# A pool for the rows of v opened ahead of the gates' pool, gathers from the seventh block on, and one low part of u in five on GpSimd

## The chip, the cores and the metric

The kernel runs on one core of a Trainium2 chip. The metric is the device time of one execution in microseconds (us); the time of the kernel before is the median of three runs. One more execution was taken by the profiler, and all rows below are from it.

## The reference

Two transformer blocks run one after the other on 512 tokens of width 1024 in fp32. The change lies in the second half of the first block, a product-key mixture of experts: each token picks 8 x 16 of 16384 single-neuron experts, weighs each expert's answer by gelu(u . h) times a softmax gate, and adds up the rows of v.

```python
def peer_ffn(h, w_query, sub_keys, peer_u, peer_v):
    ...
    idx = (jnp.take_along_axis(i1, ci // PEER_TOPK, axis=-1) * PEER_N_KEYS
           + jnp.take_along_axis(i2, ci % PEER_TOPK, axis=-1))
    g = jax.nn.softmax(sc, axis=-1)
    u_sel = peer_u[idx]
    act = jax.nn.gelu(jnp.einsum('chkd,cd->chk', u_sel, hc), approximate=False) * g
    v_sel = peer_v[idx]
    return jnp.einsum('chk,chkd->cd', act, v_sel)
    ...
```

## The kernel before

The kernel has three parts: a first mixer block, the mixture of experts (class `Peer`), and two layers of a second kind of block. The change touches only `Peer`, about 290 to 1680 us of the span.

For 384 of the 512 tokens (`ND`) the experts are computed densely, as matrix products over all 16384 experts in 128 blocks of 128 experts. For the other 128 tokens (`NGT`) the rows of u and v that a token has picked are gathered from DRAM, one gather of 128 rows of u and v for each of the 128 picks of a token.

An fp32 product is made of three products of rounded parts: an operand x is split into a high part (ScalarE, called ACT, rounds it) and a low part (x minus the high part, on VectorE, called DVE, or on GpSimd, called POOL). TensorE (PE) then multiplies high by high, high by low and low by high.

`Peer.run` opens pools one after the other. Pools are placed on a stack, so a pool that is opened after another is closed takes the same memory.

- `norm` and `route` (pool `pr`) normalize the tokens and pick the experts.
- `gates` (pool `pg`) makes a dense table of gate values. For each group of four tokens, 96 groups in all, it builds two sets of comparison matrices: `gb` (one tile for four tokens, made by DVE in two groups of three, L1774, and by GpSimd in the third, in four instructions, L1772) and `ga` (one tile for each token, made by DVE, L1784, or by ACT in two steps, L1781 and L1782). PE multiplies them (L1786, eight records in the profile for a group), ACT copies the result to `gst` (L1787), and after eight groups SP writes `gst` to DRAM (L1788), 12 times in all. `gb` has 3 buffers, `ga` 8, `gst` 2.
- `scores(b)` makes gelu(u . h) of block b for the dense tokens: SP loads `wr` (L1798), the high part `wh` is made by ACT (L1800; by DVE in one block of four from 34 on), the low part `wl` by GpSimd for b < 28 and by DVE from then on (L1802). 24 matmuls of 384 columns (L209 to L211, output `S`) follow, and ACT applies the gelu into a tile `big` (L1809), of which there are 36. 34 blocks are made ahead of the experts (`AHEAD`). Their tiles come from pools that are open all the time.
- `experts` (pool `pw`, which takes the memory of `pg`) runs over the 128 blocks: `gate(b)` loads the gates of four blocks at a time as `gt` (L1815), multiplies the scores by them on DVE (L1818) and splits the product into `ah` and `al` (L194, L195). SP loads 128 rows of v as `vr` (L1837), ACT makes `vh` (L1840), GpSimd `vl` (L1841). Then the next one or no block of scores is made, then 18 matmuls of 512 columns add to the output (L1850, output `V`), then a share of the gathers is issued: GpSimd sends the gather (L1914, `rows`, 3 buffers), DVE multiplies the u half by the token and sums (L1916), ACT and DVE make the weight (L1920, L1921), and DVE adds the v half to `acc` (L1923).

The gathers are spread evenly over the blocks up to six before the end (`LAST`): after block b, (b + 1) x 128 / 122 of them have been issued.

The order in which each engine takes its instructions is set when the program is compiled. The compiler's scheduler goes by the order of the program, but lets an engine take a later instruction whose inputs and buffers are there when an earlier one isn't ready; on the chip each engine, and each DMA queue, then keeps to that order. A tile of a pool that was opened on memory of a closed pool waits for that pool.

Of the kernel before, what the change touches and what calls it, by code (L numbers as in the profile page):

```python
# [9 lines left out]
F32 = mybir.dt.float32  # L10
F32R = mybir.dt.float32r
I32 = mybir.dt.int32
# [7 lines left out]
P = 128  # L20
D = 1024
# [235 lines left out]
class Block1:  # L257
# [29 lines left out]
    def big(self, name, dt=F32):  # L287
        return self.p.tile([P, NCH * 528], dt, tag="x16", name=self.net.nm(name), bufs=3)
# [1302 lines left out]
NG4 = ND // 32  # L1591
AHEAD = 34
LAST = 6
BIGS = 36
ON_ACT = (1,)

# [9 lines left out]
class Peer:  # L1606
# [3 lines left out]
    def run(self):  # L1610
        net, nc, tc = self.net, self.nc, self.tc
        with ExitStack() as c0:
            self.p = c0.enter_context(tc.tile_pool(name="pp", bufs=1))
            net.load_cst1(self.p, 128)
            with ExitStack() as c1:
                self.w = c1.enter_context(tc.tile_pool(name="pr", bufs=2))
                net.nsc = 3
                self.norm()
                self.route()
            with ExitStack() as c1:  # L1620
                self.w = c1.enter_context(tc.tile_pool(name="pg", bufs=2))
                self.gates()
            self.s = {}
            for b in range(AHEAD):
                self.scores(b)
            with ExitStack() as c1:
                self.w = c1.enter_context(tc.tile_pool(name="pw", bufs=2))
                self.experts()
# [99 lines left out]
    def gates(self):  # L1728

        net, nc, p, w = self.net, self.nc, self.p, self.w  # L1730
        V = nc.vector
        ident, iota = net.c("ident"), net.c("iota")
        self.gd = net.dram.tile([NG4, P, P, 32], F32, name="gates")

        g = self.sc
        gT = w.tile([P, 4, P], F32, tag="gT", name="gT", bufs=1)
        iT = w.tile([P, 2, 4, P], F32, tag="iT", name="iT", bufs=1)
        nT = w.tile([P, 2, 4, P], F32, tag="nT", name="nT", bufs=1)
        for i in range(4):
            mx = w.tile([P, 8, 1], F32, tag="rsm", name=net.nm("rmx"))  # L1740
            V.tensor_copy(mx, g[:, i, :, 0:1])
            V.tensor_tensor(g[:, i], g[:, i], mx.to_broadcast([P, 8, 16]), op=OP.subtract)
            nc.scalar.activation(g[:, i], g[:, i], AF.Exp)
            sm = w.tile([P, 8], F32, tag="rsm", name=net.nm("rsm"))
            V.tensor_reduce(sm, g[:, i], axis=AX.X, op=OP.add)
            V.reciprocal(sm, sm)
            V.tensor_tensor(g[:, i], g[:, i], sm.unsqueeze(2).to_broadcast([P, 8, 16]), op=OP.mult)
        self.g = g
        for i in range(4):
            with net.banks("pb", "gt"):  # L1750
                ps = net.ps()
            nc.tensor.transpose(ps[:, :P], g[:, i].rearrange("p a b -> p (a b)"), ident)
            nc.tensor.transpose(ps[:, P:2 * P], self.ex[:, i].rearrange("p a b -> p (a b)"), ident)
            nc.scalar.activation(gT[:, i], ps[:, :P], AF.Copy)
            xi = w.tile([P, 3, P], I32, tag="xi", name=net.nm("xi"))
            V.tensor_copy(xi[:, 0], ps[:, P:2 * P])
            V.tensor_scalar(xi[:, 1], xi[:, 0], 7, None, op0=OP.logical_shift_right)
            V.tensor_scalar(xi[:, 2], xi[:, 0], 127, None, op0=OP.bitwise_and)
            V.tensor_copy(iT[:, :, i], xi[:, 1:3])
            nc.gpsimd.tensor_scalar(nT[:, 0, i], iT[:, 0, i], -1.0, None, op0=OP.mult)  # L1760
            nc.gpsimd.tensor_scalar(nT[:, 1, i], gT[:, i], -1.0, None, op0=OP.mult)
        for t0 in range(0, ND, 32):
            st = w.tile([P, P, 32], F32, tag="gst", name=net.nm("gst"))
            for t4 in range(t0, t0 + 32, 4):
                with net.banks("pd", "G"):
                    ps = net.ps()

                i, j4 = divmod(t4, P)
                b = w.tile([P, 4, P], F32, tag="gb", name=net.nm("gb"), bufs=3)
                if t4 // 4 % 3 == 2:  # L1770
                    for t in range(4):
                        nc.gpsimd.tensor_scalar(b[:, t], iota, iT[:, 1, i, j4 + t:j4 + t + 1], None, op0=OP.is_equal)  # L1772
                else:
                    V.tensor_tensor(b, iota.unsqueeze(1).to_broadcast([P, 4, P]),  # L1774
                                    iT[:, 1, i, j4:j4 + 4].unsqueeze(2).to_broadcast([P, 4, P]), op=OP.is_equal)
                pt = ps.rearrange("p (k t) -> p t k", t=4)
                for t in range(4):
                    j = j4 + t
                    a = w.tile([P, P], F32, tag="ga", name=net.nm("ga"), bufs=8)
                    if t in ON_ACT:  # L1780
                        nc.scalar.activation(a, iota, AF.Abs, bias=nT[:, 0, i, j:j + 1])  # L1781
                        nc.scalar.activation(a, a, AF.Relu, bias=gT[:, i, j:j + 1], scale=nT[:, 1, i, j:j + 1])  # L1782
                    else:
                        V.tensor_scalar(a, iota, iT[:, 0, i, j:j + 1], gT[:, i, j:j + 1], op0=OP.is_equal,  # L1784
                                        op1=OP.mult)
                    nc.tensor.matmul(pt[:, t], b[:, t], a, start=True, stop=True)  # L1786
                nc.scalar.activation(st[:, :, t4 - t0:t4 - t0 + 4], ps.rearrange("p (k t) -> p k t", t=4), AF.Copy)  # L1787
            nc.sync.dma_start(self.gd[t0 // 32], st)  # L1788


    def big(self, dt=F32):
        return self.p.tile([P, 384], dt, tag="big", name=self.net.nm("big"), bufs=BIGS)

    def scores(self, b):

        net, nc, p = self.net, self.nc, self.p
        raw = net.wt("wr")
        nc.sync.dma_start(raw, self.A["ut"][b])  # L1798
        uh, ul = net.wt("wh"), net.wt("wl")
        (nc.vector.tensor_copy(uh, raw) if b % 4 == 3 and b >= AHEAD else nc.scalar.activation(uh, raw, AF.Copy))  # L1800
        e = nc.gpsimd if b < 28 else nc.vector
        e.tensor_tensor(ul, raw, uh.bitcast(F32), op=OP.subtract)  # L1802
        with net.banks("pa", "S"):
            ps = net.ps()[:, :ND]
        for c in range(NCH):
            cs = slice(c * P, (c + 1) * P)
            net.mm3(ps, (uh[:, cs], ul[:, cs]), (self.xh[c][:, :ND], self.xl[c][:, :ND]), c == 0, c == NCH - 1)
        self.s[b] = self.big()[:, :ND]
        nc.scalar.activation(self.s[b], ps, AF.Gelu)  # L1809
# [15 lines left out]
    def experts(self):  # L1825

        net, nc, w, hT = self.net, self.nc, self.w, self.hT
# [4 lines left out]
        done, got = AHEAD, 0  # L1832
        slots = NGT
        for b in range(P):
            ah, al = self.gate(b)
            raw = w.tile([P, D], F32, tag="vr", name=net.nm("vr"), bufs=2)
            nc.sync.dma_start(raw, self.A["uv"][b * P:(b + 1) * P, D:])  # L1837
            vh = w.tile([P, D], F32R, tag="vh", name=net.nm("vh"), bufs=2)
            vl = w.tile([P, D], F32R, tag="vl", name=net.nm("vl"), bufs=2)
            nc.scalar.activation(vh, raw, AF.Copy)  # L1840
            nc.gpsimd.tensor_tensor(vl, raw, vh.bitcast(F32), op=OP.subtract)  # L1841
            while done < min(P, AHEAD + (b + 1) * (P - AHEAD) // (P - LAST)):
                self.scores(done)
                done += 1
            for i, ps in enumerate(out):
                ts = slice(i * P, (i + 1) * P)
                for k in range(2):
                    cs = slice(k * 512, (k + 1) * 512)
                    for n, (x, y) in enumerate(((ah, vh), (ah, vl), (al, vh))):
                        nc.tensor.matmul(ps[k], x[:, ts], y[:, cs], start=b == 0 and n == 0, stop=b == P - 1 and n == 2)  # L1850
            n = min(slots, (b + 1) * slots // (P - LAST)) - got
            while n > 0:
                self.gather(got, min(n, 3))
                got, n = got + min(n, 3), n - 3
# [123 lines left out]
```

## Time and profile before

| | us |
|---|---|
| median of three runs | 3770.8 |
| the three runs | 3761.55, 3776.63, 3770.8 |
| the profiled execution, its own time | 3765.66 |
| its span, from the first to the last instruction | 3763.8 |

| engine | busy us | share of the span |
|---|---|---|
| PE, matmuls | 3593.1 | 95% |
| PE, weight loads | 2972.0 | 79% |
| DVE | 2592.4 | 69% |
| ACT | 1412.5 | 38% |
| POOL | 1087.1 | 29% |

The profile is one execution taken by the hardware's profiler. Busy time of PE is modelled and overlaps, so a busy PE need not be at its peak. "PEclk" is the clock granted to PE as a share of the full clock, and "DMA" the mean busy share of the core's 16 DMA engines. A row that ends in "<-" and a name tells how long the engine stood idle before an instruction and what ended the idle time.

### The profile page before, as it was taken

What the parts mean: (1) busy time and instruction counts of PE and PEld (TensorE: products, weight loads), DVE (VectorE), ACT (ScalarE), POOL (GpSimd) and SP (SyncE); (2) the same over time, 40 slices, a digit from 0 to 9 for tenths busy, and PEclk for the clock granted to TensorE, in tenths of its full rate; (3) what the DMA queues carried; (4) which work ended last, traced back from release to release, by engine and by line L of the source; (5) the groups of instructions that cost most, each with busy time, mean ns of one, the idle gap of its engine ahead of it and who ended that gap; (6) DMA issues with size and microseconds to landing.
All of it is one profiled execution on the core that took longest, in us unless ns stands there. A gap on an engine that the chain in (4) does not pass through costs nothing. (4 is left out here: it accounts for less than half of the span.)

```text
span 3763.8 us, 46084 instructions
## 1 busy us (share of the span) xinstructions
PE 3593.1 (95%) x17229; PEld 2972.0 (79%) x17229; DVE 2592.4 (69%) x4504; ACT 1412.5 (38%) x2405; POOL 1087.1 (29%) x685
## 2 busy tenths in 40 slices
PE   7798979889999999999999899999999998999999
PEld 6656878878889988888887667888888875668887
DVE  9668999788888889854445987444444459975443
ACT  3253259423333333342223446322322234453222
POOL 4424767445555555530002222000100012210000
PEclk8899989999999999999999999999999999999999
DMA  4212225888888888833223111323332321112233
GB/s 119 78 40 94 76 91 224 284 304 295 286 307 292 301 291 297 301 111 95 93 98 94 64 46 56 96 95 95 96 95 95 98 93 54 46 45 95 95 96 101
DMA packets 181520, 529.88 MB, mean 141 GB/s; under 512 B 22256, under 2 KB 73008, under 8 KB 163120
## 3 DMA queue, kind: packets, MB, share of 16 engines
q1 hardware_dynamic: 157504, 388.64, 31.0%
q0 software_dynamic: 19392, 136.06, 9.8%
q10 hardware_dynamic: 4400, 2.24, 0.3%
q8 instruction: 136, 2.23, 0.2%
q14 instruction: 88, 0.72, 0.1%
HBM read 495.52 MB, written 30.18 MB: 140 GB/s over the span
## 5 line engine op out<-in xcount | busy, mean ns | idle before, releaser
L1027 ACT ACTIVATE wh<-wr 128x1024 fp32r<-128x1024 f32 (+1 forms) x334 | 347.4, 1040 | 1029.8 <-PE ps L210 766.0
L210 PE MATMUL ps<-x,wh 128*128 128x512 f32 x1408 | 548.8, 390 | 2.1 <-DVE x L996 2.0
L209 PE MATMUL ps<-x,wh 128*128 128x512 f32 x1408 | 549.1, 390 | 0.0
L211 PE MATMUL ps<-x,wl 128*128 128x512 f32 x1408 | 547.9, 389 | 0.0
L1028 DVE TENSOR_TENSOR wl<-wr,wh 128x1024 fp32r<-128x1024 f32 (+1 forms) x288 | 344.4, 1196 | 78.0 <-ACT wh L1027 71.1
L1008 POOL TENSOR_TENSOR s<-s,s 128x512 f32<-128x512 f32 x42 | 67.0, 1596 | 1125.2 <-ACT s L1006 1113.9
L1841 POOL TENSOR_TENSOR vl<-vr,vh 128x1024 fp32r<-128x1024 f32 x128 | 325.4, 2543 | 183.3 <-ACT vh L1840 178.2
L211 PE MATMUL S<-x,wl 128*128 128x384 f32 x1024 | 349.7, 341 | 8.1 <-POOL wl L1802 8.1
L209 PE MATMUL S<-x,wh 128*128 128x384 f32 x1024 | 349.4, 341 | 0.0
L210 PE MATMUL S<-x,wh 128*128 128x384 f32 x1024 | 348.6, 340 | 0.0
L1850 PE MATMUL V<-vl,ah 128*128 128x512 f32 x768 | 302.7, 394 | 12.0 <-POOL vl L1841 12.0
L210 PEld LDWEIGHTS ps<-x,wh 128*128 128x128 f32 x1408 | 264.3, 188 | 61.4 <-DVE x L996 5.9
L1850 PE MATMUL V<-vh,ah 128*128 128x512 f32 x768 | 300.7, 393 | 10.1 <-ACT vh L1840 10.1
L209 PEld LDWEIGHTS ps<-x,wh 128*128 128x128 f32 x1408 | 264.2, 188 | 55.8 <-issue 1.0
L211 PEld LDWEIGHTS ps<-x,wl 128*128 128x128 f32 x1408 | 264.3, 188 | 54.7
L1850 PE MATMUL V<-vh,al 128*128 128x512 f32 x768 | 302.5, 394 | 1.3 <-DVE al L195 1.3
L211 PE MATMUL ps<-ml,wl 128*128 128x512 f32 x704 | 278.1, 395 | 0.0
L209 PE MATMUL ps<-ml,wh 128*128 128x512 f32 x704 | 278.0, 395 | 0.0
L1914 POOL DMA_INDIRECT rows<-in_uv_dram,gidx x128 | 188.1, 1470 | 260.9 <-DVE acc L1923 230.9
L1055 DVE TENSOR_TENSOR s<-ps,rs 128x512 f32<-128x512 f32 x88 | 60.8, 691 | 278.8 <-PE ps L211 278.8
L1067 DVE SCALAR_TENSOR_TENSOR hT<-ps,hT 128x512 f32<-128x512 f32 x96 | 66.3, 691 | 270.7 <-PE ps L211 270.7
L1802 DVE TENSOR_TENSOR wl<-wr,wh 128x1024 fp32r<-128x1024 f32 x100 | 186.9, 1869 | 63.8 <-ACT wh L1800 63.7
(582 smaller groups left out, 7936.7 us busy)
## 6 DMA issues: line engine op xcount, KB each, us to landing
wr<-in_f_gu_dram SPq DMA_DIRECT2D x176, 512.0 KB, 3.7
wr<-in_ut_dram SPq DMA_DIRECT2D x128, 512.0 KB, 5.3
vr<-in_uv_dram SPq DMA_DIRECT2D x128, 512.0 KB, 4.8
wr<-in_f_dn_dram SPq DMA_DIRECT2D x64, 448.0 KB, 3.3
gates<-gst SPq DMA_DIRECT2D x12, 2048.0 KB, 6.8
gt<-gates SPq DMA_DIRECT2D x32, 768.0 KB, 7.3
wr<-in_w_dram SPq DMA_DIRECT2D x46, 512.0 KB, 3.4
wr<-in_f_dn_dram SPq DMA_DIRECT2D x32, 512.0 KB, 3.6
```

The source lines that it names most:

```text
L209: mm(out, wh, xh, start=start, stop=False)
L210: mm(out, wh, xl, start=False, stop=False)
L211: mm(out, wl, xh, start=False, stop=stop)
L1008: nc.gpsimd.tensor_tensor(sq, acc, sq, op=OP.add)
L1027: nc.scalar.activation(hi, raw, AF.Copy)
L1028: (eng or nc.vector).tensor_tensor(lo, raw, hi.bitcast(F32), op=OP.subtract)
L1055: V.tensor_mul(u, ps[1], r)
L1067: V.scalar_tensor_tensor(x[:, m], ps, 0.5, x[:, m], op0=OP.mult, op1=OP.add)
L1802: e.tensor_tensor(ul, raw, uh.bitcast(F32), op=OP.subtract)
L1841: nc.gpsimd.tensor_tensor(vl, raw, vh.bitcast(F32), op=OP.subtract)
L1850: nc.tensor.matmul(ps[k], x[:, ts], y[:, cs], start=b == 0 and n == 0, stop=b == P - 1 and n == 2)
L1914: nc.gpsimd.indirect_dma_start(r, None, self.A["uv"], bass.IndirectOffsetOnAxis(ap=self.gi[:, s:s + 1], axis=0))
```

## The change

Five edits, all in `Peer`:

- a pool `pv` with two buffers for each tile is opened after `route` and before the gates' pool, and stays open through the experts; the tiles `vr`, `vh` and `vl` (24 KB of each partition) come from it and no longer from `pw`;
- in the gates, `xi` has 1 buffer instead of 2, `gb` 2 instead of 3, `ga` 7 instead of 8;
- the low part of u is made by GpSimd also for every fifth block from 30 on (30, 35, ... 125);
- the gathers start with the seventh block: after block b, (b - 5) x 128 / 116 of them have been issued, none before;
- a constant `FIRST = 6` for that.

```diff
+FIRST = 6
...
                 self.norm()
                 self.route()
+
+            self.pv = c0.enter_context(tc.tile_pool(name="pv", bufs=2))
             with ExitStack() as c1:
                 self.w = c1.enter_context(tc.tile_pool(name="pg", bufs=2))
                 self.gates()
...
-            xi = w.tile([P, 3, P], I32, tag="xi", name=net.nm("xi"))
+            xi = w.tile([P, 3, P], I32, tag="xi", name=net.nm("xi"), bufs=1)
...
-                b = w.tile([P, 4, P], F32, tag="gb", name=net.nm("gb"), bufs=3)
+                b = w.tile([P, 4, P], F32, tag="gb", name=net.nm("gb"), bufs=2)
...
-                    a = w.tile([P, P], F32, tag="ga", name=net.nm("ga"), bufs=8)
+                    a = w.tile([P, P], F32, tag="ga", name=net.nm("ga"), bufs=7)
...
-        e = nc.gpsimd if b < 28 else nc.vector
+        e = nc.gpsimd if b < 28 or b % 5 == 0 else nc.vector
...
-            raw = w.tile([P, D], F32, tag="vr", name=net.nm("vr"), bufs=2)
+            raw = self.pv.tile([P, D], F32, tag="vr", name=net.nm("vr"))
             nc.sync.dma_start(raw, self.A["uv"][b * P:(b + 1) * P, D:])
-            vh = w.tile([P, D], F32R, tag="vh", name=net.nm("vh"), bufs=2)
-            vl = w.tile([P, D], F32R, tag="vl", name=net.nm("vl"), bufs=2)
+            vh = self.pv.tile([P, D], F32R, tag="vh", name=net.nm("vh"))
+            vl = self.pv.tile([P, D], F32R, tag="vl", name=net.nm("vl"))
...
-            n = min(slots, (b + 1) * slots // (P - LAST)) - got
+            n = min(slots, max(0, b + 1 - FIRST) * slots // (P - LAST - FIRST)) - got
```

## Rows read from the trace of the kernel before

**Rows 1.** The page, part 1: busy time and share of the span, by engine.

```profile
PE 3593.1 (95%) x17229; PEld 2972.0 (79%) x17229; DVE 2592.4 (69%) x4504; ACT 1412.5 (38%) x2405; POOL 1087.1 (29%) x685
```

**Rows 2.** Stretches: bounds, length, busy PE, PEld, DVE, ACT, POOL, clock, DMA, GB/s.

```profile
600.00:640.00 40.00, 36.88 (x274) 35.34 (x273) 36.93 (x93) 36.09 (x83) 33.53 (x37) 1.00 0.51 204
710.00:720.00 10.00, 7.69 (x25) 6.62 (x26) 10.00 (x12) 3.94 (x8) 5.34 (x2) 0.64 0.83 246
740.00:760.00 20.00, 17.21 (x80) 14.02 (x78) 19.39 (x27) 6.40 (x12) 11.53 (x7) 1.00 1.02 357
760.00:800.00 40.00, 31.45 (x138) 26.42 (x138) 35.71 (x43) 10.22 (x18) 17.85 (x9) 0.91 0.88 291
900.00:1600.00 700.00, 699.21 (x3476) 628.36 (x3475) 608.16 (x657) 239.90 (x416) 388.76 (x197) 1.00 0.83 297
```

**Rows 3.** Waits of 696 to 900 us: us in total, times, longest.

```profile
PE V L1850 <- POOL vl L1841: 11.2, 6, 4.0
...
PE V L1850 <- ACT vh L1840: 10.1, 1, 10.1
```

**Rows 4.** Order of time, 685 to 713 us, by engine: start, duration, instruction [idle before].

```profile
685.05 0.32 SPq L1788 DMA_DIRECT2D gates<-gst  x1
...
691.99 0.96 POOL L1906 MEMSET acc<- 128x1024 f32 x1 [8.63 <-DMA gates<-gst]
693.31 1.08 POOL L1914 DMA_INDIRECT rows<-in_uv_dram,gidx  x1 [0.36 <-DVE gidx L1882]
...
693.02 1.21 SPq L1815 DMA_DIRECT2D gt<-gates  x1
694.28 8.17 SPq L1837 DMA_DIRECT2D vr<-in_uv_dram  x2
...
709.24 1.49 DVE L1818 TENSOR_TENSOR big<-big,gt 128x384 f32<-128x384 f32 x3 [10.05 <-DMA gt<-gates]
...
711.21 1.99 ACT L1840 ACTIVATE vh<-vr 128x1024 fp32r<-128x1024 f32 x2
...
712.31 2.50 PE L1850 MATMUL V<-vh,ah 128*128 128x512 f32 x5 [10.10 <-ACT vh L1840]
```

**Rows 5.** DMA: sends with median landing (684:720, 720:800, 900:1600); gathers' queue, 720:800.

```profile
gates<-gst SPq DMA_DIRECT2D x1, 2048.0 KB, 6.8
...
q0 software_dynamic: 1440, 10.49, 34.0%
...
gt<-gates SPq DMA_DIRECT2D x9, 768.0 KB, 7.0
...
gt<-gates SPq DMA_DIRECT2D x18, 768.0 KB, 7.1
```

**Rows 6.** Instructions by line, 526 to 686 us: busy, mean ns | idle before.

```profile
L1772 POOL TENSOR_SCALAR gb<-cst,iT 128x128 f32<-128x128 f32 x128 | 94.4, 752 | 32.2 <-PE G L1786 32.2
```

**Rows 7.** Order of time in the gate stage: GpSimd, DVE, PE.

```profile
605.45 2.69 POOL L1802 TENSOR_TENSOR wl<-wr,wh 128x1024 fp32r<-128x1024 f32 x1
...
605.85 2.38 DVE L1784 TENSOR_SCALAR ga<-cst,iT,gT 128x128 f32<-128x128 f32 x1
...
624.72 1.05 PE L1786 MATMUL G<-ga,gb 128*128 128x128 f32 x8
```

**Rows 8.** Single lines: ns min/median/max, first and last start; idle of L1786's engine until.

```profile
L1798 SPq DMA_DIRECT2D wr<-in_ut_dram x128: 327/328/2085, 291.6 to 1593.3; - x128
...
L1802 DVE TENSOR_TENSOR wl<-wr,wh x100: 1207/1220/3984, 644.6 to 1610.9; 128x1024 fp32r<-128x1024 f32 x100
...
L1841 POOL TENSOR_TENSOR vl<-vr,vh x128: 2345/2419/3425, 712.3 to 1648.3; 128x1024 fp32r<-128x1024 f32 x128
...
L1784 DVE TENSOR_SCALAR ga<-cst,iT,gT x288: 328/336/2398, 527.1 to 682.8; 128x128 f32<-128x128 f32 x144
...
  POOL gb L1772: 0.5, 3
```

**Rows 9.** Waits of 900 to 1600 us: us in total, times, longest.

```profile
PEld V L1850 <- POOL vl L1841: 1.6, 2, 0.9
```

## The prediction

> **What bounds the kernel now.** I read the shares of the engines first, then the stretches of the mixture-of-experts part, then the waits of the bad stretch, then its order of time. PE is busy 95% of the span [rows 1], so a change of DVE's, ACT's or GpSimd's load only pays where PE waits. From 900 to 1600 us it does not wait: 699.21 of 700 us, with DVE at 608, GpSimd at 389 and the DMA engines at 0.83 [rows 2]. There 3476 matmuls take 699.21 us, 0.201 us each; one v block (18) with one u block (24) is 8.4 us. This stretch can only lose.
>
> The loss lies at the seam between the gates and the experts, 700 to 800 us. In 696 to 900 PE waited 10.1 us once for the high part of v and 11.2 us in six waits for its low part [rows 3]. After the long wait the granted clock falls to 0.64 of full speed in 710 to 720, so some 7.2 us ran at the lower of the two levels (1.2 of 2.4 GHz); 2.3 us of that slice are idle, so about (7.2 - 2.3) / 2 = 2.4 us of work time is lost. In 760 to 800 (0.91) 7.2 us ran at that level and 8.5 us were idle; I put the loss at 1.5, between 0 and 3.6 [rows 2]. All that can be had is 10.1 + 11.2 + 2.4 + 1.5 = **25.2 us**.
>
> Why it is lost is seen in the order of time [rows 4]. At 693.02 SP sends the first load of gates and at 694.28 the first two of v, which take 8.17 us to send; GpSimd sends three gathers from 693.31. The first use of the gates comes at 709.24, 16.2 us after the send, where the usual landing is 7.1 [rows 5]. ACT makes the high part of v only at 711.21, and PE goes on at 712.31. GpSimd's clearing of the accumulator, which needs no gate, waited 8.63 us for the last gates to be written: tiles of the later pool wait for the whole earlier pool, the v rows too. After that the DMA engines are full (1.02 in 740 to 760 [rows 2]): the gathers' queue alone takes 34% of them from 720 to 800, and nine loads of gates come in these 80 us where the steady stretch has 18 in 700 [rows 5].
>
> **The change part by part.** *The pool of v.* Nothing is added or removed on PE. The first two loads of v no longer wait for the gates' pool; they can go when the router's pool is free, and that the program's order allows this is seen on the first load of u, which goes at 291.6, long before the gates [rows 8]. Off the seam come two loads on SP (8.17 us), two conversions on ACT (1.99) [rows 4] and two subtractions on GpSimd of 2.42 [rows 8]. They land in the gate stage, where they are not free: see below. At the seam the gates alone end last: written 6.8 us after 685.05, sent at 693.0, landed 7.1 later [rows 4, 5], then the product on DVE and a rounding on ACT, about 1 us together: 701.1. PE is through at 702.2 (712.31 - 10.10). So the whole 10.1 and the 2.4 of clock go, unless the gates end later.
>
> *Fewer buffers for the gates.* gb goes from 3 to 2, ga from 8 to 7, xi from 2 to 1; this pays for the room. GpSimd makes every third gb, 32 blocks in 94.4 us (2.95 each), and between them waits 32.2 us for PE, about 1.0 a block [rows 6]. With three buffers its buffer is always its own and it waits for its own group; with two it shares both, and in strict order it waits until the next group has left PE, one group of eight matmuls, 1.05 us [rows 7], more. Ends: 0 (a buffer goes to whoever asks first, so that GpSimd keeps one and DVE's 0.7 us copies rotate in the other) and 32 x 1.05 = 34 us. In 600 to 640 DVE is busy 36.9, ACT 36.1 and PE 36.9 of 40 [rows 2], so little slack takes this up. Yet PE waited for GpSimd's gb only 0.5 us in three waits [rows 8], the nearest row, so I take the low end, with 3 us.
>
> The two subtractions fall here too. While one such subtraction ran at 605.45, a DVE product that takes 0.34 us by its median [rows 8] took 2.38 [rows 7]; two of them are 0 to 4.8 us, I take 2. Together the gates end 5 us later, 0 to 39.
>
> The Trainium skill, SBUF — State Buffer, section Who interferes with whom, says the same in general: GpSimd and DVE share a port pair under an exclusive lock, and the one that comes second stands still for the whole instruction. The trace agrees (2.38 against 0.34 us); by this rule alone both subtractions would block DVE, 4 us instead of 2.
>
> A later end of the gates costs less than its length if PE has other work: blocks 34 and 35 of u need no gate (36 buffers of scores), 48 matmuls of 0.201, 9.7 us. Whether they stand ahead of the first v block in PE's order I can't see; half of the time is my guess. With 5 us later the start gains 5 to 10; I take 7 of 10.1 + 2.4.
>
> *No gather beside six blocks.* 128 gathers go over 116 blocks instead of 122, 5% denser; for the first six blocks, some 45 to 50 us, GpSimd, DVE and the 34% of DMA are free. What is late next there is the loads of gates, nine in 80 us; without the gathers DMA stands near 0.65, which holds them. Of the 11.2 + 1.5 and the rest of the clock (2.4 if not yet counted) I take 13, ends 3 (the full DMA moves to block 6) and 15. The denser gathers add nothing on PE while it is saturated.
>
> *One low part in five on GpSimd.* Blocks 30, 35, ... 125, 20 of them: DVE loses 20 x 1.22 = 24 us, GpSimd gains 20 x 2.42 = 48 [rows 8], from 389 to some 430 in the 700 us. Behind such a subtraction stand, in GpSimd's queue, the next low part of v and the next gather. The same operation for v, in the same queue, cost PE 1.6 us in two waits over 700 us [rows 9]; the cost is 0, ends -1 and 48 (each fully exposed). This is worth nothing by itself: DVE is not late there.
>
> **Sum.** 7 + 13 - 0 = **20 us** off the profiled execution, 3765.7 (span 3763.8 and 1.9 around it): 3745.7. The median of the three runs, 3770.8, stands 5.1 above it, so I predict **3751**.
>
> **The rivals.**
> 1. *The gate stage gets longer, and eats the start.* Gates 20 us later (0.6 of a group for each GpSimd block): the start then loses about 10, the rest still gives 13: gain 3, 3768, with 3760 to 3773 around it. For it: three engines above 90% there [rows 2]; against: PE hardly waited for gb.
> 2. *The ring of two buffers is strict (the slow side).* Each of GpSimd's 32 blocks waits a group more, and both subtractions block DVE: 39 us, so PE would start on v at about 741 instead of 712.3: -29 + 13 = -16, 3787; with one u matmul or two in between each time (0.2 to 0.4 x 32) it is 3790 to 3800. It decides from 23 us later on, where start and rest cancel. For it: GpSimd's wait of 1.0 follows each of its blocks now [rows 6]. Against: DVE's gb need 0.7 us and could take turns in one buffer.
> 3. *The crowd moves.* Gathers begin at block 6 while the gate loads still come ahead of their blocks, and DMA is full then instead. Only 4 of the 13 come: 7 + 4 = 11, 3760.
> 4. *It all goes and the gates don't move:* 10 + 15 to 17, 3744.
> 5. *The pool does nothing*, because the compiler's order leaves the v loads behind the gates: then 10.1 stays and the gate stage still has fewer buffers; the time is that of the first rival, and I count it there.
>
> **How the numbers follow.** Forecast 0.53 (its own range 3744 to 3756), first rival 0.20, second 0.10, third 0.12, fourth 0.05. About 0.5%, 18.9 us, is what a measurement of this kernel can tell from no change: the line is at 3752. Of the forecast 0.42 lies below it and 0.11 within. Faster: 0.42 + 0.05 = 0.47; same: 0.11 + 0.20 + 0.12 = 0.43; slower 0.10. The range takes all but the second rival and the thin lower end: 3738 to 3774.
>
> **What would show it.** Right: the first v load sent before 640 us; no gather sent before the seventh block; the first gates landed within 8 us of their send; PE's wait at the seam under 4 us, with the granted clock at 1.00 behind it; its waits for the low part of v in the hundred us after it under 3 us; GpSimd's wait for PE in the gate stage near 32 us, and the last write of gates at 685 to 692. Wrong: gates written after 700; GpSimd waiting 50 us and more for PE; DMA still at 1.0 after block 6; or PE waiting for the low part of u in the steady stretch, which would break the 8.4 us for a pair of blocks.

## The result and the profile after

The changed kernel is slower: 3824.91 us (median of four runs, 3822.53 to 3828.13) against 3772.02 (four runs), a ratio of 1.0145 with a 95% interval of 1.0122 to 1.0167. The forecast was 3751, with a range up to 3774.

| | before | after | more |
|---|---|---|---|
| start of the span to the first v matmul | 712.3 | 732.7 | 20.4 |
| first to last v matmul | 942.0 | 968.7 | 26.7 |
| from there to the end of the span | 2109.5 | 2124.8 | 15.3 |
| span of the profiled execution | 3763.8 | 3826.2 | 62.4 |

The profiled execution of the changed kernel, 3828.13, is the highest of its four; that of before, 3765.66, lies below three of before's four: the medians differ by 52.9. The table comes from the span and from the first and last start of the v matmuls (line L1850 before, L1853 after; ns min/median/max, then first and last start):

```profile
L1850 PE MATMUL V<-vh,ah x768: 387/389/796, 712.3 to 1654.3; 128*128 128x512 f32 x192
```

```profile
L1853 PE MATMUL V<-vh,ah x768: 387/389/632, 732.7 to 1701.4; 128*128 128x512 f32 x192
```

The first row of the table has three parts. GpSimd's first step of the gate stage comes at 520.61, 4.4 us earlier than before (525.05); from there to the last send of gates it takes 196.2 us instead of 160.0; from that send to the first v matmul 15.9 instead of 27.3.

Busy time after, by engine (answers to [rows 1]): PE's share is the same, DVE has 55 us more, although some of its work was given to GpSimd, and GpSimd (POOL) has 58 more.

```profile
PE 3615.9 (95%) x17229; PEld 2974.5 (78%) x17229; DVE 2647.1 (69%) x4478; ACT 1411.5 (37%) x2399; POOL 1144.7 (30%) x705
```

Stretches of the changed kernel, columns as in [rows 2]. In the gate stage all engines do less in the same time, so none of them is the limit; from 900 to 1600 us PE, full before, now lacks 17 of 700 us, and DVE is busy 641 us instead of 608 with fewer instructions (633 instead of 657).

```profile
600.00:640.00 40.00, 34.26 (x237) 30.66 (x236) 32.55 (x81) 30.69 (x68) 25.48 (x32) 1.00 0.46 181
...
760.00:800.00 40.00, 31.09 (x141) 26.62 (x140) 22.05 (x33) 7.55 (x13) 14.49 (x6) 0.87 0.75 230
900.00:1600.00 700.00, 682.57 (x3343) 606.72 (x3342) 640.61 (x633) 224.71 (x397) 416.44 (x206) 0.99 0.82 292
```

**The gate stage.** GpSimd's comparison matrices in order of time; each row is four instructions, the bracket is the time that GpSimd stood idle before them and who ended it. Starts are 4.9 us apart with 1.95 of waiting between. GpSimd's four before these end at 615.01; PE then multiplies that group and the next one (the row of PE, whose end is modelled), and GpSimd goes on at 616.96: it waits for one group beyond its own.

```profile
615.96 1.18 PE L1789 MATMUL G<-ga,gb 128*128 128x128 f32 x8
...
616.96 2.98 POOL L1775 TENSOR_SCALAR gb<-cst,iT 128x128 f32<-128x128 f32 x4 [1.95 <-PE G L1789]
621.89 2.98 POOL L1775 TENSOR_SCALAR gb<-cst,iT 128x128 f32<-128x128 f32 x4 [1.95 <-PE G L1789]
```

By line over the whole stage (522 to 718 us), the answer to [rows 6]: idle time before them went from 32.2 to 60.2 us; 45.2 of it is put down to PE, for 11.4 ("issue") the profile shows no one.

```profile
L1775 POOL TENSOR_SCALAR gb<-cst,iT 128x128 f32<-128x128 f32 x128 | 91.3, 727 | 60.2 <-PE G L1789 45.2 <-issue 11.4 <-PE S L209 1.8
```

**The early v work.** In order of time, 516 to 549 us: the v loads do go at 516, and their subtractions stand on GpSimd at the start of the gate stage. Behind the second stands a low part of u, and GpSimd's next comparison matrices start 9.9 us after the last ones, not 4.9.

```profile
516.07 0.80 SPq L1840 DMA_DIRECT2D vr<-in_uv_dram  x2
...
533.50 2.78 POOL L1805 TENSOR_TENSOR wl<-wr,wh 128x1024 fp32r<-128x1024 f32 x1
...
536.75 2.36 POOL L1805 TENSOR_TENSOR wl<-wr,wh 128x1024 fp32r<-128x1024 f32 x1
539.08 2.37 POOL L1844 TENSOR_TENSOR vl<-vr,vh 128x1024 fp32r<-128x1024 f32 x1
543.69 2.45 POOL L1775 TENSOR_SCALAR gb<-cst,iT 128x128 f32<-128x128 f32 x4 [2.24 <-PE G L1789]
546.11 2.64 POOL L1844 TENSOR_TENSOR vl<-vr,vh 128x1024 fp32r<-128x1024 f32 x1
548.71 2.36 POOL L1805 TENSOR_TENSOR wl<-wr,wh 128x1024 fp32r<-128x1024 f32 x1
553.56 2.64 POOL L1775 TENSOR_SCALAR gb<-cst,iT 128x128 f32<-128x128 f32 x4 [2.49 <-PE G L1789]
```

**The seam**, the answer to [rows 4]. The last gates are sent 31.7 us later than before (716.79 against 685.05). From there the way is short: gates loaded at 724.20, used at 730.87, PE on v at 732.73 after 0.89 us of waiting (10.10 before). A gather is sent at 725.68 all the same, but 1.5 us behind the load of gates, where before it was 0.3 us.

```profile
716.79 0.32 SPq L1791 DMA_DIRECT2D gates<-gst  x1
...
724.20 1.26 SPq L1818 DMA_DIRECT2D gt<-gates  x2
...
725.68 1.08 POOL L1917 DMA_INDIRECT rows<-in_uv_dram,gidx  x1 [0.36 <-DVE gidx L1885]
...
730.87 2.19 DVE L1821 TENSOR_TENSOR big<-big,gt 128x384 f32<-128x384 f32 x3 [1.66 <-DMA gt<-gates]
...
732.73 0.50 PE L1853 MATMUL V<-vh,ah 128*128 128x512 f32 x1 [0.89 <-ACT ah L194]
```

**The first v blocks.** Waits of 740 to 900 us (us, times, longest) and the worst place of them in order of time. DVE waits 26.4 us for loads of gates; behind these waits, in its queue, is the product of the first gather, for which ACT waits 11.93 us with the rounding of v behind it; then GpSimd, then PE.

```profile
DVE big L1821 <- DMA gt<-gates: 26.4, 6, 12.8
...
PE V L1853 <- POOL vl L1844: 12.1, 7, 5.5
```

```profile
770.63 0.20 ACT L1923 ACTIVATE dot<-dot 128x1 f32<-128x1 f32 x1 [11.93 <-DVE rows L1919]
...
772.27 6.01 POOL L1844 TENSOR_TENSOR vl<-vr,vh 128x1024 fp32r<-128x1024 f32 x1 [14.91 <-ACT vh L1843]
...
778.33 0.80 PE L1853 MATMUL V<-vl,ah 128*128 128x512 f32 x1 [5.52 <-POOL vl L1844]
```

**The steady stretch.** One place. While GpSimd makes a low part of u (948.68), DVE's product with a gathered row takes 3.41 us (its median from 850 to 1640 us is 1.22). ACT waits 6.31 us for it; the rounding of v stands behind that in ACT's queue, and PE waits 1.51 us for the high part of v. GpSimd, which has sent a gather at 951.42, itself stands idle 0.85 us for that high part, makes the low part of v at 954.04, and PE waits 1.98 us for it.

```profile
948.68 2.59 POOL L1805 TENSOR_TENSOR wl<-wr,wh 128x1024 fp32r<-128x1024 f32 x1
951.42 1.77 POOL L1917 DMA_INDIRECT rows<-in_uv_dram,gidx  x1
954.04 2.40 POOL L1844 TENSOR_TENSOR vl<-vr,vh 128x1024 fp32r<-128x1024 f32 x1 [0.85 <-ACT vh L1843]
...
948.94 3.41 DVE L1919 SCALAR_TENSOR_TENSOR rows<-rows,hn 128x1024 f32<-128x1024 f32 x1
...
952.39 0.20 ACT L1923 ACTIVATE dot<-dot 128x1 f32<-128x1 f32 x1 [6.31 <-DVE rows L1919]
...
954.01 0.51 PE L1853 MATMUL V<-vh,ah 128*128 128x512 f32 x1 [1.51 <-ACT vh L1843]
...
956.49 0.50 PE L1853 MATMUL V<-vl,ah 128*128 128x512 f32 x1 [1.98 <-POOL vl L1844]
```

Followed back one by one, PE's 20 waits from 850 to 1640 us (21.7 us) are of two main kinds. Thirteen of them (13.7 us) go through ACT as here: ACT had stood 4.5 to 9.3 us for DVE's product with a gathered row, and GpSimd was not late: it waited for ACT as well, or PE waited for the high part itself. Only six (6.5 us) end with GpSimd's own queue, each time a low part of u and a gather ahead of the low part of v. DVE got no relief from the work it gave away. Its product of scores and gates, before and after, from 900 to 1600 us (busy time, mean ns, idle before):

```profile
L1818 DVE TENSOR_TENSOR big<-big,gt 128x384 f32<-128x384 f32 x74 | 52.7, 712 | 4.7 <-ACT big L1809 4.7
```

```profile
L1821 DVE TENSOR_TENSOR big<-big,gt 128x384 f32<-128x384 f32 x70 | 91.5, 1307 | 14.8 <-ACT big L1812 14.8
```

### The profile page after: what moved, and what is told of

Its sections match the earlier page's. It is cut to its first block, busy times and chain, and to the rows that moved or that the text cites. A ratio compares the mean times of both kernels' runs of the same rounds, so it can differ in the third digit from the quotient of the medians.

```text
span 3826.2 us, 46091 instructions
## 1 busy us (share of the span) xinstructions
PE 3615.9 (95%) x17229; PEld 2974.5 (78%) x17229; DVE 2647.1 (69%) x4478; ACT 1411.5 (37%) x2399; POOL 1144.7 (30%) x705
## 5 line engine op out<-in xcount | busy, mean ns | idle before, releaser
L1853 PE MATMUL V<-vl,ah 128*128 128x512 f32 x768 | 305.7, 398 | 27.0 <-POOL vl L1844 27.0
L1853 PE MATMUL V<-vh,ah 128*128 128x512 f32 x768 | 302.2, 393 | 5.4 <-ACT vh L1843 4.5
L1853 PE MATMUL V<-vh,al 128*128 128x512 f32 x768 | 304.5, 397 | 2.1 <-DVE al L195 1.9
L1028 POOL TENSOR_TENSOR wl<-wr,wh 128x1024 fp32r<-128x1024 f32 x46 | 116.8, 2540 | 378.0 <-ACT wh L1027 361.4
```

The source lines that it names most:

```text
L1028: (eng or nc.vector).tensor_tensor(lo, raw, hi.bitcast(F32), op=OP.subtract)
```

## The experiments

The changed kernel has three parts that can be tried apart: the pool of v with the cut buffers, the moved gathers, and the low parts of u on GpSimd. The theory after the result was: the ring of two gb buffers is what lengthens the gate stage (the second rival of the prediction), and GpSimd's longer queue is what lengthens the v blocks. The second half of this holds only in part, as the stretch above shows. Times are medians, beside those of the kernel before on the same chip.

### The cut buffers alone

```diff
-xi = w.tile([P, 3, P], I32, tag="xi", name=net.nm("xi"))
+xi = w.tile([P, 3, P], I32, tag="xi", name=net.nm("xi"), bufs=1)
...
-b = w.tile([P, 4, P], F32, tag="gb", name=net.nm("gb"), bufs=3)
+b = w.tile([P, 4, P], F32, tag="gb", name=net.nm("gb"), bufs=2)
...
-a = w.tile([P, P], F32, tag="ga", name=net.nm("ga"), bufs=8)
+a = w.tile([P, P], F32, tag="ga", name=net.nm("ga"), bufs=7)
```

> The kernel before with the gates' buffers alone cut (gb 2, ga 7, xi 1); pools, gathers and low parts as before. Theory ring: with two gb buffers GpSimd waits for one more group of PE, so the last write of gates is sent at about 716 us instead of 685, and, as the loads of v still wait for the gates, PE starts on v some 31 us later than 712: the whole is 25 to 35 us slower than before, about 3800. Rival load: the gates end late in the changed kernel because the first loads and subtractions of v were moved into the gate stage; then this kernel has its last write at 685 to 690 and is within 8 us of before.

3789.24 against 3770.40, ratio 1.0047 (1.0030 to 1.0064), 18.8 us slower. The writes of gates (first and last send) and the v matmuls:

```profile
L1788 SPq DMA_DIRECT2D gates<-gst x12: 326/326/327, 552.7 to 711.9; - x12
```

```profile
L1850 PE MATMUL V<-vh,ah x768: 387/389/628, 729.7 to 1673.9; 128*128 128x512 f32 x192
```

The gates end 26.9 us later with no v work in the stage: the theory of the ring holds. But v starts only 17.4 us later, less than the 31 expected. In this run the first load of gates got ahead of the gathers (sent at 719.21, first gather at 720.57) and was used at 726.43, 7.2 us later instead of 16.2.

### The moved gathers alone

```diff
+FIRST = 6
...
-n = min(slots, (b + 1) * slots // (P - LAST)) - got
+n = min(slots, max(0, b + 1 - FIRST) * slots // (P - LAST - FIRST)) - got
```

> The kernel before with the gathers alone moved (none beside the first six blocks, 5% denser after). Theory subtractions (PE waits in the steady stretch because of the low parts of u that GpSimd makes): no new waits for the low part of v after 850 us (under 6 us, as before), the full DMA after 712 us is gone or moved, 0 to 15 us faster than before, 3757 to 3772. Rival gathers (the denser gathers hold GpSimd's queue, so PE waits for v): 10 to 25 us of waits for the low part of v after 850 us, and 0 to 15 us slower than before.

3777.32 against 3770.40, ratio 1.0018 (1.0008 to 1.0028). The weight loads of the v matmuls waited 14.7 us for the low part of v from 850 to 1640 us, 3.1 in the kernel before (us, times, longest; before, then this run):

```profile
PEld V L1850 <- POOL vl L1841: 3.1, 4, 1.1
```

```profile
PEld V L1851 <- POOL vl L1842: 14.7, 17, 1.6
```

So gathers 5% denser make PE wait, each time about a microsecond: the rival holds here, though not alone (next run). PE itself waited 16 times in that stretch, 9.3 us; 12 of these waits (8.0 us) go through ACT and DVE as above, so it isn't GpSimd's queue that they end with. Right behind the seam the moved gathers do help: PE's waits for the low part of v from 696 to 900 us, 11.2 before [rows 3], are

```profile
PE V L1851 <- POOL vl L1842: 2.9, 2, 2.5
```

### The low parts of u on GpSimd alone

```diff
-e = nc.gpsimd if b < 28 else nc.vector
+e = nc.gpsimd if b < 28 or b % 5 == 0 else nc.vector
```

> The kernel before with one low part of u in five made by GpSimd from block 30 on, nothing else. Theory subtractions: PE's waits for the low part of v after 850 us rise from 5 to 20 us or more, and the kernel is 15 to 25 us slower, about 3790. Rival gathers: waits stay under 8 us and the time within 6 us of before.

3780.80 against 3770.40, ratio 1.0029 (1.0019 to 1.0040), 10.4 us slower, less than expected. The v blocks take 955.4 us from first to last matmul (709.5 to 1664.9), 13.4 more than before, and the same wait is

```profile
PEld V L1850 <- POOL vl L1841: 12.2, 12, 2.5
```

Both theories of the steady stretch hold as to the part that does it: each alone adds 9 to 12 us of waits for the low part of v.

### The pool of v with the cut buffers, without the other two

The edits are against the changed kernel.

```diff
-e = nc.gpsimd if b < 28 or b % 5 == 0 else nc.vector
+e = nc.gpsimd if b < 28 else nc.vector
...
-n = min(slots, max(0, b + 1 - FIRST) * slots // (P - LAST - FIRST)) - got
+n = min(slots, (b + 1) * slots // (P - LAST)) - got
```

> The changed kernel with the gathers as before and all low parts of u from block 28 on made by DVE: the pool of v and the cut buffers are left. Theory ring: last write of gates sent at 712 to 720 us, PE starts on v at 730 to 735, 20 us later than before, and the full DMA after it costs what it cost before: 18 to 25 us slower than before, about 3793; with the first kernel of this batch it shows what the pool gives back, about 10 us. Rival load: last write 715 and the first kernel of this batch at 688.

3797.56 against 3770.40, ratio 1.0067 (1.0050 to 1.0084), 27.2 us slower.

```profile
L1791 SPq DMA_DIRECT2D gates<-gst x12: 320/326/383, 561.1 to 721.1; - x12
```

Beside the first run only the pool differs: the last write is 9.2 us later (721.1 against 711.9) and the first already 8.4 later (561.1 against 552.7). GpSimd's first step of the stage comes 0.8 us later too (525.10 against 524.28). So the early v work costs 8.4 us, nearly all of it at the very start of the gate stage, where the rows above show the two subtractions. PE starts on v at 736.0, 14.9 us behind the last send, 17.8 in the first run: the pool gives back 3 us of these 8, not the 10 expected.

### Two gb buffers alone, and seven ga buffers alone

```diff
-b = w.tile([P, 4, P], F32, tag="gb", name=net.nm("gb"), bufs=3)
+b = w.tile([P, 4, P], F32, tag="gb", name=net.nm("gb"), bufs=2)
```

> The kernel before with gb cut from 3 to 2 buffers and nothing else. Theory ring: this one buffer is the whole loss of the gate stage; the last write of gates is sent at 708 to 714 us (685 before), GpSimd's blocks of four gb instructions start 4.7 to 5 us apart, some 18 us slower than before. Rival ga: the seventh ga buffer does it; then the last write is at 685 to 690 here.

```diff
-a = w.tile([P, P], F32, tag="ga", name=net.nm("ga"), bufs=8)
+a = w.tile([P, P], F32, tag="ga", name=net.nm("ga"), bufs=7)
```

> The kernel before with ga cut from 8 to 7 buffers and nothing else. Theory ring: last write of gates at 683 to 690 us, time within 6 us of before. Rival ga: last write at 705 or later.

One run each: 3792.91 and 3763.99, against 3770.44. The writes of gates, with two gb and then with seven ga, and GpSimd's order of time with two gb:

```profile
L1788 SPq DMA_DIRECT2D gates<-gst x12: 326/326/327, 553.2 to 714.0; - x12
```

```profile
L1788 SPq DMA_DIRECT2D gates<-gst x12: 319/320/424, 546.4 to 683.8; - x12
```

```profile
642.00 2.85 POOL L1772 TENSOR_SCALAR gb<-cst,iT 128x128 f32<-128x128 f32 x4 [1.96 <-PE G L1786]
646.80 2.49 POOL L1772 TENSOR_SCALAR gb<-cst,iT 128x128 f32<-128x128 f32 x4 [1.95 <-PE G L1786]
```

The one gb buffer is the whole loss of the gate stage that the cut buffers bring, and the starts are 4.8 us apart, as expected; 22 us slower is a little more than the 18 expected. The ga buffer costs nothing that can be seen. In its run the three gathers at the seam happened to go 1.4 us behind the first load of gates (693.31 against 691.94), not 0.3, and the gates were used 8.2 us after their send; PE started on v at 705.0, 7.3 us earlier than before, with no pool of v at all.

### The changed kernel with the third gb buffer

```diff
-BIGS = 36
+BIGS = 35
...
-b = w.tile([P, 4, P], F32, tag="gb", name=net.nm("gb"), bufs=2)
+b = w.tile([P, 4, P], F32, tag="gb", name=net.nm("gb"), bufs=3)
...
-a = w.tile([P, P], F32, tag="ga", name=net.nm("ga"), bufs=7)
+a = w.tile([P, P], F32, tag="ga", name=net.nm("ga"), bufs=6)
```

> The changed kernel with the third gb buffer back; the room for it is taken from ga (6) and from the score tiles (35 instead of 36). Theory ring: last write of gates at 690 to 698 us (717 in the changed kernel; a few us above 685 because the two early subtractions of v still stand in the gate stage), PE starts on v at 705 to 713, 20 to 27 us faster than the changed kernel, about 3800, and still slower than before by the gathers and the subtractions. Rival: if the early v work is what fills GpSimd, the last write stays above 708.

3784.90 against 3770.44, ratio 1.0037 (1.0025 to 1.0050).

```profile
L1791 SPq DMA_DIRECT2D gates<-gst x12: 326/327/384, 560.2 to 696.3; - x12
```

The gates end 20.5 us earlier than in the changed kernel and v starts at 710.7 instead of 732.7: as expected. The time is 40 us below the changed kernel's median, more than the 20 to 27 expected; 15.5 of the 42.7 us by which the two profiles differ lie behind the experts, see the last run.

### The pool alone, with three gb buffers

The kernel of the run just above, with the gathers and the low parts of u as before.

```diff
-e = nc.gpsimd if b < 28 or b % 5 == 0 else nc.vector
+e = nc.gpsimd if b < 28 else nc.vector
...
-n = min(slots, max(0, b + 1 - FIRST) * slots // (P - LAST - FIRST)) - got
+n = min(slots, (b + 1) * slots // (P - LAST)) - got
```

> The pool of v alone, with three gb buffers (ga 6, xi 1, 35 score tiles), gathers and low parts of u as before. Theory: the gates end 5 to 9 us later through the early v work, the way from the last write to PE's start on v shrinks from 27 us to 15 to 18: between 8 us faster and 4 us slower than before, 3762 to 3774. Rival: the pool itself is what costs; then more than 8 us slower.

3770.34 against 3770.44, ratio 0.9999 (0.9989 to 1.0008): no difference. The last gates are sent at 695.7, some 10 us later than before, and v starts at 709.4, 13.7 us behind that (27.3 before). What the pool saves at the seam it takes in the gate stage. And some of what it saves there is the order of sends: here too the load of gates goes 1.4 us ahead of the first gather (702.99 and 704.38), and the run with seven ga buffers has 21.2 us from the last send to v without the pool.

### The gathers held back in fact

The compiler's order sends the first three gathers at the seam even where the source has none beside six blocks, because their three buffers and their indices are there. Here the indices are made to depend on the sixth block's scores; 0.0 times the scores changes no value.

```diff
+FIRST = 6
...
 ah, al = self.gate(b)
+if b == FIRST - 1:
+    V.scalar_tensor_tensor(self.gi, ah[:, :P].bitcast(F32), 0.0, self.ex[:, 3].rearrange("p a b -> p (a b)"), op0=OP.mult, op1=OP.add)
...
-n = min(slots, (b + 1) * slots // (P - LAST)) - got
+n = min(slots, max(0, b + 1 - FIRST) * slots // (P - 2 - FIRST)) - got
...
-V.tensor_copy(idx, self.ex[:, 3].rearrange("p a b -> p (a b)"))
```

> The kernel before with the gathers from the seventh block on, spread to the last but one (1.067 a block; 1.049 before, 1.103 in the changed kernel), and their indices made to depend on the gated scores of the sixth block, so that no gather can be sent at the seam. Theory hoist: the three gathers that the compiler's order sends at 692 us whatever the source says crowd the first loads of gates and v; without them the first gates land within 8 us, PE starts on v at 701 to 706 instead of 710 to 712, and the kernel is 4 to 12 us faster than the one of this batch without the hold. Rival: the loads of gates and v crowd each other without the gathers; then PE's start stays at 709 or later.

3767.78 against 3771.58, ratio 0.9989 (0.9978 to 1.0000). The first load of gates, its first use and the first gather, in order of time:

```profile
693.26 1.09 SPq L1816 DMA_DIRECT2D gt<-gates  x1
...
700.98 1.50 DVE L1819 TENSOR_TENSOR big<-big,gt 128x384 f32<-128x384 f32 x3 [1.55 <-DMA gt<-gates]
...
742.81 1.14 POOL L1916 DMA_INDIRECT rows<-in_uv_dram,gidx  x1 [1.83 <-DVE gidx L1838]
```

### The same spread without the hold

```diff
+FIRST = 6
...
-n = min(slots, (b + 1) * slots // (P - LAST)) - got
+n = min(slots, max(0, b + 1 - FIRST) * slots // (P - 2 - FIRST)) - got
```

> The kernel before with the gathers from the seventh block on, spread to the last but one: 1.067 a block instead of the 1.103 of the run with the gathers alone moved. Theory density: PE's waits for the low part of v after 850 us fall from 15 us to 8 or less, and the time is 3 to 8 us below that run, about 3771. Rival position: the waits stay at 12 to 16 us, because the moved start and not the density makes them.

3771.11 against 3771.58, ratio 0.9993 (0.9982 to 1.0003). The first use of the gates, and the wait of 850 to 1640 us:

```profile
706.30 1.50 DVE L1819 TENSOR_TENSOR big<-big,gt 128x384 f32<-128x384 f32 x3 [9.63 <-DMA gt<-gates]
```

```profile
PEld V L1851 <- POOL vl L1842: 9.0, 9, 2.6
```

Held back, the gates are used 7.7 us after their load is sent and v starts at 704.1; without the hold it is 15.8 us (sent at 690.51) and 709.4. So the gathers that the compiler sends early (hoists) are what crowds the first load of gates, as expected. The v blocks, however, take 947.2 us with the hold and 939.2 without: what is won at the seam is lost again in the v blocks, and the two medians differ by 3.3 us, under the 4 to 12 expected. Of density: 1.049, 1.067 and 1.103 gathers a block give waits of 3.1, 9.0 and 14.7 us. That goes with density, as expected, if not all the way down to 8; from the first to the second the start of the gathers moves too.

### Moved gathers and low parts of u together, no pool

The kernel before with the diffs of the second and the third run.

```diff
+FIRST = 6
...
-e = nc.gpsimd if b < 28 else nc.vector
+e = nc.gpsimd if b < 28 or b % 5 == 0 else nc.vector
...
-n = min(slots, (b + 1) * slots // (P - LAST)) - got
+n = min(slots, max(0, b + 1 - FIRST) * slots // (P - LAST - FIRST)) - got
```

> The kernel before with both the moved gathers and the low parts of u on GpSimd, without the pool and with all buffers. Theory sum: the loss of PE after the first 150 us of the v blocks is near 30 us, as in the changed kernel and more than the 15 and 12 of each alone, as both lengthen GpSimd's one queue; some 22 us slower than before, about 3792. Rival: the changed kernel's 30 needs the pool; then the loss here is 22 to 24.

One run, 3791.03 against 3771.58. The v blocks take 966.1 us (707.6 to 1673.7), 24.1 more than before, and the wait is

```profile
PEld V L1851 <- POOL vl L1842: 23.3, 18, 2.8
```

The changed kernel has 25.1 in the same stretch. The steady loss needs neither the pool nor the cut buffers, and the two parts add up. That DVE's longer instructions make part of it is not shown by a run: none of them changes these alone.

### The changed kernel once more

> The changed kernel once more, to see the part behind the experts a second time: it took 2124 us from the last v matmul on in the profile, 2109 before, with the same instructions in the same order on each engine. If the order of events in the changed kernel makes it longer, it is 2120 or more again; if it is spread between executions, it lies at 2108 to 2117, as in the other runs.

One run, 3818.07 against 3771.58. The gates end at 720.1, v starts at 735.7 and lasts 962.4 us (735.7 to 1698.1). Behind the last v matmul, stretches of the kernel before, of the changed kernel and of this run (columns as in [rows 2]):

```profile
1655.00:3764.00 2109.00, 2051.64 (x9189) 1622.91 (x9187) 1204.25 (x1847) 755.69 (x1188) 196.79 (x106) 0.99 0.26 83
```

```profile
1702.00:3826.00 2124.00, 2059.18 (x9189) 1626.14 (x9188) 1202.22 (x1847) 756.93 (x1188) 207.33 (x106) 0.99 0.26 83
```

```profile
1698.60:3816.00 2117.40, 2056.87 (x9190) 1622.94 (x9188) 1203.26 (x1847) 755.99 (x1188) 202.46 (x106) 0.99 0.26 83
```

Measured as in the first table it is 2118.0, between what was set for the two theories. The other runs above have 2109 to 2123 here (2109.3 with three gb and the whole change, 2122.8 with the gathers spread), with the same instructions in the same order on each engine. So at least part of the 15 us of the first table is spread between executions; whether the changed kernel is long here for a reason of its own stays open.

## Why the prediction was wrong

**The seam, as far as it was read, came out right, in part by luck.** The v loads went at 516, before 640; the first gates were used 6.7 us after their load; PE's wait of 10.1 fell to 0.9. From the last send to PE on v the terms gave 16 us; 15.9 were measured. But the terms took it that no gather would be sent there. Gathers were sent, 1.5 us behind the load of gates. In the runs without the pool such a lead was enough (7.2 to 8.2 us from the send to the first use), and one of 0.2 or 0.3 us was not (13 to 16).

**The step that failed first is the price of the buffers.** I gave 0 and 34 us as ends and took 3, by the row in which PE waited 0.5 us for GpSimd's gb. That was the wrong row. In a ring the late engine's waits are seen on the other side: it was GpSimd that stood idle 32.2 us [rows 6], and what had to be asked of that row was what one more group per turn would do. It went to 60.2, 28 more, close to 32 x 1.05 = 34; the last write moved by 26.9 (all three buffers cut) and 28.9 us (gb alone). The second rival, 0.10 of the chance, had the mechanism and the price of the stage (39 us with the early v work, 36.2 measured). Its time of 3787 was still 38 us short, as it counted on the 13 us of the gathers and on a steady stretch that loses nothing; that the buffers alone measured 3789 to 3793 is a coincidence. That a buffer would go to whoever asks first did not happen: GpSimd waited 1.95 us at each turn of the rows above.

**The early v work** was priced at 2 us, ends 0 and 4.8; it cost 8.4. I priced what DVE and GpSimd cost each other on single instructions, and left out that the subtractions stand in the ring itself: GpSimd's queue holds two low parts of u, a low part of v, and only then the next gb, and behind that one a low part of v and one of u.

**The gathers beside six blocks** failed in two ways. They were not held back: the first went at 725.68, since the compiler's order sends what has buffers and indices. The sentence that GpSimd, DVE and 34% of DMA would be free for 45 to 50 us rests on the source, not on the order. And where they were held back, the v blocks took longer (947.2 against 939.2 us): that is the outcome of the third rival, though no row here shows that full DMA engines made it. In the changed kernel the 12.1 us of waits of 740 to 900 are as large as the 11.2 of [rows 3]; at their worst place DVE's wait for loads of gates, with a gather's product behind it, now ends last. Of the 13 us that I took nothing came there. With the gathers alone moved 8.3 us did come (11.2 to 2.9), and the denser gathers took them back later.

**The steady stretch** was to lose nothing, with -1 and 48 as the ends for the low parts of u and no cost for denser gathers. Alone they cost 10.4 and 6.9 us of time, together about 20, and the v blocks of the changed kernel grew by 26.7. The row I priced by, 1.6 us in two waits over 700 [rows 9], says how often the low part of v was late with the load there was, not what more load does. I looked at GpSimd's 389 of 700 us and not at what it shares with DVE and ACT. The term by which DVE loses 24 us was wrong: DVE was busy 32 us longer from 900 to 1600, since its instructions took longer beside GpSimd's subtractions. ACT waits for DVE's products with gathered rows, the rounding of v stands behind that, and GpSimd comes last in this chain; 13.7 of PE's 21.7 us went this way, 6.5 through GpSimd's queue alone. "The denser gathers add nothing on PE while it is saturated" is the sentence that the density runs refute.

**The sum** by parts, from the medians: buffers 18.8, pool on top of them 8.3 (3797.56 - 3789.24), gathers 6.9, low parts of u 10.4, in all 44.4; measured 52.9 by the medians, and 46.5 by the one later run (3818.07 - 3771.58). Of the rest, 2 to 8.5 us, the gathers and the low parts together cost 2 more than their sum (one run), and the part behind the experts may hold the remainder; that is not shown. A kernel with three gb buffers and the pool alone is level with the one before, and none of these runs beats it by more than the measurement can tell.

## What to carry to other kernels

Before a buffer is taken out of a ring that several engines fill, look at the producer's waits for the consumer, not at the consumer's waits for the producer: a producer that waits after each of its turns is in the loop already, and here the buffer less cost about one turn of the consumer each time. Work moved onto an engine that is half busy delays what stands behind it in its queue, and need not relieve the engine it was taken from; where the next link waits for both, a bound engine with no slack pays for each delay. Follow a wait back past the engine that ended it: that one may have been waiting too. Whether a source edit holds a transfer back is a matter of what it depends on: where a buffer is free, a compiler's order may send it anyway.

## What the runs showed of the hardware

- A load of gates (768 KB in pieces of 512 bytes, sent by SP) was used 15.5 to 16.2 us after its send where three gathers followed, the first 0.3 us behind it (three runs), and about 13 us where two followed that closely (two runs). With the first gather 1.4 us behind it took 7.2 to 8.2 us without the early v loads, and 5.2 to 6.7 us where these were already there; with no gather 7.7 us.
- From 900 to 1600 us of the changed kernel 92 instructions of DVE took at least 0.4 us longer than their like mostly do, and all 92 ran beside a subtraction on GpSimd; before it was 90 of 90. In all DVE's instructions were longer by some 231 us, before by 178.
- The stretch behind the experts, with the same instructions in the same order, lasted 2109 to 2125 us in the profiled executions, and the changed kernel alone 2118 and 2125: some 15 us, 0.4% of the whole, that no part of the change was shown to cause.
